# Residual rows and result kept with channels as rows, and parameter rows packed into two loads, in a two-layer diffusion backbone

## Chip, cores and metric

The kernel runs on one core of one Trainium2 chip. The metric is the device time of the core in microseconds (us) for one execution. The kernel before was timed in three runs: their median is 1773.47 us, the lowest 1773.41 and the highest 1774.19. One more execution was recorded by the hardware profiler: it took 1773.3 us.

## What is computed

The reference is a diffusion backbone of two layers over 512 latent tokens `x` (1, 512, 1024) with 256 context tokens `ctx` (1, 256, 1024). Cut to what matters:

```
for layer in 0, 1:
    mod, mod_c = silu(c) @ ada_w + ada_b, silu(c_ctx) @ ada_w + ada_b   # shift, scale, gate: twice 3 x 1024
    hx = rms_norm(x, norm1_g) * (1 + sc1) + sh1                          # hc alike, from ctx and mod_c
    yx, yc = windowed_gqa(hx, hc) if layer == 0 else hgrn2_bidir(hx, hc)
    x  = x + g1 * yx                                                     # the residual
    hx2 = rms_norm(x, norm2_g) * (1 + sc2) + sh2
    x  = x + g2 * conv_glu(hx2)                                          # 1024 -> 2 x 2816 -> 1024
    ctx = the same two steps, in layer 0 only
return x                                                                 # (1, 512, 1024)
```

Layer 0 mixes by attention: 16 heads in 4 groups, a window of 128 tokens on each side and all context keys in one softmax with a sink. Layer 1 mixes by a gated linear recurrence in both directions. All data is float32.

## The kernel before

**Layout.** TensorE contracts over the 128 partitions, so activations are kept with channels as partitions: the residual is `xl`, 8 channel tiles of 128 x 512 latent tokens, and `xc`, 8 tiles of 128 x 256 context tokens. `x` and `ctx` come, and the result goes, with tokens as rows, so three places of the program turn 128 x 128 blocks: PE multiplies the block with an identity (`ident`, the first half of the constant tile `cst`; the second half, `ones`, is a matrix of ones), and ACT or DVE copies the turned block from PSUM.

**Products.** For precision each float32 weight tile is split into a high and a low part: ACT writes the high part `wh` (L118, L142), DVE the rest, `wl` (L119, L143). Each product is then three matmuls (high by high, high by low, low by high), issued by `mm_steps` (L177), by `product` (L195) and, for the projections of attention, at L634.

**Start (`setup` from L199, `load_params`, `first_norm`).** ACT's queue loads `cst`. SP's queue loads six token tiles of 128 tokens x 1024 channels (L483: four of `x`, two of `ctx`). After the first of them `load_params` is called: it loads the rows of the small parameters (`c`, `c_ctx`, two norm gains, biases, convolution weights) into a tile `rows` by eleven DMAs, three on SP (L221 to L223) and eight on ACT (L224 to L230). Then SP loads 32 tiles `ar` of the modulation weights, 256 KB each (L303), and among these the weights `wr` of the key and value projection. The parameter rows are turned into columns (`par`), the conditioning `cs` is made of `c`, and PE works out the first modulation products (`ada`, L282). The token tiles are normalized in place. Then `flip` (L515) turns them, 6 blocks for each of the 8 channel tiles, 48 blocks in all (products named `n`), a modulation makes `hn` of them (L355 is one of its steps), and the first product that uses `hn` is `kv`.

**Attention.** For each of 4 groups and 6 query tiles: scores `S` on PE (L814), row maximum on DVE, exponential on ACT (L820), row scale `P` on POOL (L822), transposes `pt` on PE (L872), the products `pv` with the values (L882), and a copy to `o` on ACT (L884). Other projections are laid between these steps.

**Attention output (`attn_out` from L928).** For each pair of channel tiles d and d + 4 the two weight tiles are loaded and split. For each d, the 128 channels d of `x` and `ctx` are loaded a second time, with tokens as rows, into a tile `xs` (L937 and L938, on ACT's queue, in rows of 512 bytes), PE turns 6 blocks (L941, `xT`), ACT copies them to `xl` and `xc` (L943), and then come the 48 pairs of matmuls of the output projection `ao` (each pair 512 and 256 tokens wide). DVE adds the result, times the gate, onto `xl` and `xc` (L955). The attention output `oh` is itself split before (ACT L893, DVE L894). PSUM holds two tiles for `xT` and two for `ao`, each of two banks.

**Middle.** The convolutional GLU of layer 0, the recurrence of layer 1 and the second GLU follow, untouched by the change. The last products of the second GLU are `dn` (L177), which DVE adds onto `xl` (L1116; the last channel tile is added in two halves, L1111).

**Result (`done1`).** As each channel tile of `xl` is final, PE turns its four blocks (L1551; for the last channel tile two blocks for each half, L1543), ACT copies them from PSUM (L1552, L1544), and SP stores them with tokens as rows: three stores of two channel tiles each, one of one tile, and two halves of the last (L1556, L1554, L1545).

**What sets the order.** The program is written in the order above, but a list scheduler lays the instructions out anew for each engine, by a simulated timeline and by priorities; the order of rows below is its outcome. Each engine then executes its instructions in that order, and an instruction that waits holds all behind it. The DMAs of SP and ACT are instructions in their streams. Each DMA takes one of eight completion semaphores (DMAHW0 to DMAHW7 in the rows) in turn, and a DMA whose semaphore is still owed by an earlier DMA waits until that one has landed.

Of the kernel before, what the change touches and what calls it, by code (L numbers as in the profile page):

```python
# [8 lines left out]
F32 = mybir.dt.float32  # L9
# [64 lines left out]
class Kernel:  # L74
# [135 lines left out]
    def load_params(self, es):  # L210
# [5 lines left out]
        q = nc.scalar  # L216

        def rowsrc(x):
            return x.rearrange("l (r p) -> (l r) p", p=P)
# [5 lines left out]
        q.dma_start(out=rows[48:64, 0, :], in_=rowsrc(a["hgrn_lb_logits"]))  # L225
        q.dma_start(out=rows[64:65, 0, :], in_=rowsrc(a["hgrn_o_gain"]))
        q.dma_start(out=rows[0:96, 1, :], in_=rowsrc(a["ada_b"]))
        for l in range(2):
            q.dma_start(out=rows[0:66, 2 + l, :], in_=a["ffn_conv_w"][l].rearrange("w (r p) -> (w r) p", p=P))
            q.dma_start(out=rows[66:88, 2 + l, :], in_=a["ffn_conv_b"][l:l + 1].rearrange("w (r p) -> (w r) p", p=P))  # L230
# [239 lines left out]
    def first_norm(self, es, hn, psR, tables, after):  # L470
# [9 lines left out]
        for i in range(6):  # L480
            x = xp.tile([P, D], F32, tag="x", name=f"x{i}")
            src = a["x"][0, i * P:(i + 1) * P, :] if i < 4 else a["ctx"][0, (i - 4) * P:(i - 3) * P, :]
            nc.sync.dma_start(out=x, in_=src)  # L483
            xs.append(x)
            if i == 0:
                self.load_params(es)
# [441 lines left out]
    def attn_out(self, oh, hs, acc, tmp, pj, pp):  # L928
        nc, a = self.nc, self.a
        wout = a["attn_w_out"][0]  # L930
        for dp in range(KT // 2):
            w = self.load_w([self.wcols(wout, d * P, P) for d in (dp, dp + 4)])
            for j in range(2):
                d = dp + 4 * j
                xs = tmp.tile([P, 6, P], F32, tag="xs", name="xs")
                cs = slice(d * P, (d + 1) * P)
                nc.scalar.dma_start(out=xs[:, 0:4], in_=a["x"][0, :, cs].rearrange("(t p) c -> p t c", p=P))  # L937
                nc.scalar.dma_start(out=xs[:, 4:6], in_=a["ctx"][0, :, cs].rearrange("(t p) c -> p t c", p=P))  # L938
                pt = pp.tile([P, 1024], F32, tag="p2", name="xT")
                for i in range(6):  # L940
                    nc.tensor.transpose(pt[:, i * P:(i + 1) * P], xs[:, i], self.ident)  # L941
                for lo, hi, x in self.segs(False):
                    nc.scalar.activation(x[:, d], pt[:, lo:hi], AF.Copy)  # L943
# [485 lines left out]
    def run(self, stop=99):  # L1429
# [33 lines left out]
        with ExitStack() as e2:  # L1463
            pp, pj = (_Turn([self.pool(e2, f"{n}{i}", 1, PSUM) for i in range(2)]) for n in ("ppA", "pjA"))
            xsp = self.pool(e2, "xsp", 2)
            self.attn_out(oh, hs, acc, _Multi(tmp, xsp, ("xs",)), pj, pp)
# [67 lines left out]
        ost = {}  # L1534

        def done1(d, bank, part=None):

            if d == KT - 1:
                n = LAT // 2
                pt = bank("xo")  # L1540
                o = gp.tile([P, 2, P], F32, tag="g", name="osl")
                for i in range(2):
                    nc.tensor.transpose(pt[:, i * P:(i + 1) * P], self.xl[:, d, part * n + i * P:part * n + (i + 1) * P], self.ident)  # L1543
                nc.scalar.activation(o, pt[:, :n].rearrange("p (i c) -> p i c", c=P), AF.Copy)  # L1544
# [78 lines left out]
```

## Time and profile before

| | |
|---|---|
| median of three runs | 1773.47 us |
| profiled execution | 1773.3 us |
| span of its instructions | 1771.5 us |
| PE busy | 1742.6 us (98%), 13033 matmuls |
| DVE busy | 1308.5 us (74%) |
| ACT busy | 833.6 us (47%) |
| POOL busy | 247.3 us (14%) |
| DMA | 166.44 MB, 94 GB/s on average |

All times in the rows of the profile are microseconds from the first instruction; the span ends with the last one, and the execution's own time is 1.8 us longer. PE is the matrix engine, DVE the vector engine, ACT the scalar engine, POOL the GpSimd engine and SP an engine that only issues DMAs. `L515` is line 515 of the kernel before. Four kinds of rows are shown further on:

- A row of the chain or of the timeline: start, duration, engine, what was made, line, number of instructions in the row. The chain is followed back from the last instruction, at each step to what released it, or to the instruction before it on its engine. In a timeline the brackets at the end hold the idle time before the row and what ended it.
- A row of the windows: a stretch, its length, then for PE, PE's weight loads, DVE, ACT and POOL the busy time (and how many instructions), then the granted clock of PE (1.00 is full speed), the sum of the DMA engines' busy shares, and GB/s.
- A row of the groups: line, engine, operation, tile, count, then the mean, median and longest duration in ns, and when.
- A row of the waits: who waits for what, the time in sum, how often, the longest.

### The profile page before, as it was taken

What the parts mean: (1) busy time and instruction counts of PE and PEld (TensorE: products, weight loads), DVE (VectorE), ACT (ScalarE), POOL (GpSimd) and SP (SyncE); (2) the same over time, 40 slices, a digit from 0 to 9 for tenths busy, and PEclk for the clock granted to TensorE, in tenths of its full rate; (3) what the DMA queues carried; (4) which work ended last, traced back from release to release, by engine and by line L of the source; (5) the groups of instructions that cost most, each with busy time, mean ns of one, the idle gap of its engine ahead of it and who ended that gap; (6) DMA issues with size and microseconds to landing.
All of it is one profiled execution on the core that took longest, in us unless ns stands there. A gap on an engine that the chain in (4) does not pass through costs nothing.

```text
span 1771.5 us, 32299 instructions
## 1 busy us (share of the span) xinstructions
PE 1742.6 (98%) x13033; PEld 1528.3 (86%) x13033; DVE 1308.5 (74%) x2394; ACT 833.6 (47%) x1740; POOL 247.3 (14%) x232
## 2 busy tenths in 40 slices
PE   5999999999999999999999999999999999999998
PEld 4967775789889888999999889999897899999997
DVE  6576677477777776867867767777776699999984
ACT  4355556565534443534455333333333465565553
POOL 1133333200100110100100101111110001111110
PEclk9999999999999999999999999999999999999999
DMA  9351005133333343213114212121225423333311
GB/s 309 110 198 42 24 2 191 52 92 113 122 120 99 123 139 96 87 42 99 54 52 117 62 45 61 53 57 40 58 73 190 123 72 105 110 105 108 91 59 66
DMA packets 205188, 166.44 MB, mean 94 GB/s; under 512 B 5406, under 2 KB 199023, under 8 KB 199919
## 3 DMA queue, kind: packets, MB, share of 16 engines
q1 hardware_dynamic: 197376, 160.47, 29.5%
q10 hardware_dynamic: 7662, 3.92, 0.8%
q8 instruction: 102, 1.67, 0.4%
q14 instruction: 48, 0.39, 0.1%
HBM read 162.27 MB, written 2.10 MB: 93 GB/s over the span
## 4 chain that ended last, share of the span: by engine, by line
PE 96%; DMA 2%; DVE 1%; ACT 0%; issue 0%; POOL 0%; SPq 0%; ACTq 0%; DVEq 0%
PE dn L177 17%; PE pZ L195 17%; PE pV L195 8%; PE pf L177 8%; PE pY L195 4%; PE pjq L634 4%; PE pv L177 4%; PE ao L177 4%; PE pv L882 3%; PE pgate L177 3%; PE pq L177 3%; PE pt L872 3%; PE ada L316 2%; PE kv L634 2%; PE pd L969 2%; PE S L814 2%
## 5 line engine op out<-in xcount | busy, mean ns | idle before, releaser
L195 PE MATMUL pZ<-hs,wh 128*128 128x386 f32 (+1 forms) x1312 | 296.7, 314 | 0.0
L177 PE MATMUL dn<-g,wh 128*128 128x512 f32 (+1 forms) x1062 | 268.0, 356 | 0.0
L142 ACT ACTIVATE wh<-wr 128x512 fp32r<-128x512 f32 x246 | 153.7, 629 | 242.7 <-PE pZ L195 89.2
L118 ACT ACTIVATE wh<-wr 128x512 fp32r<-128x512 f32 (+2 forms) x204 | 120.2, 603 | 271.5 <-PE pf L177 82.1
L195 PEld LDWEIGHTS pZ<-hs,wh 128*128 128x128 f32 x1312 | 224.1, 189 | 14.8 <-ACT wh L142 5.9
L143 DVE TENSOR_TENSOR wl<-wr,wh 128x512 fp32r<-128x512 f32 x246 | 182.5, 746 | 35.8 <-ACT wh L142 31.6
L195 PE MATMUL pZ<-hs,wl 128*128 128x386 f32 (+1 forms) x656 | 204.7, 313 | 0.0
L177 PEld LDWEIGHTS dn<-g,wh 128*128 128x128 f32 x1062 | 174.7, 189 | 25.7 <-ACT g L1062 0.3
L119 DVE TENSOR_TENSOR wl<-wr,wh 128x512 fp32r<-128x512 f32 (+2 forms) x204 | 140.4, 695 | 74.3 <-ACT wh L118 65.1
L992 POOL TENSOR_TENSOR gg<-gg,R 128x772 f32<-128x772 f32 (+1 forms) x41 | 85.3, 2079 | 715.2 <-DVE gg L991 626.0
L177 PE MATMUL dn<-g,wl 128*128 128x512 f32 (+1 forms) x531 | 162.1, 355 | 0.0
L195 PE MATMUL pV<-hs,wh 128*128 128x386 f32 (+1 forms) x656 | 148.6, 313 | 0.0
L195 PEld LDWEIGHTS pZ<-hs,wl 128*128 128x128 f32 x656 | 123.4, 188 | 0.1
L177 PE MATMUL pf<-hn,wh 128*128 128x512 f32 (+1 forms) x512 | 117.7, 344 | 0.6 <-DVE gate L1160 0.6
L195 PEld LDWEIGHTS pV<-hs,wh 128*128 128x128 f32 x656 | 111.9, 189 | 1.3 <-issue 0.8
L195 PE MATMUL pV<-hs,wl 128*128 128x386 f32 (+1 forms) x328 | 102.2, 313 | 0.0
L177 PEld LDWEIGHTS dn<-g,wl 128*128 128x128 f32 x531 | 89.4, 188 | 14.2
L1116 DVE SCALAR_TENSOR_TENSOR xl<-dn,mod,xl 128x512 f32<-128x512 f32 x95 | 70.5, 745 | 29.6 <-PE dn L177 29.5
L177 PEld LDWEIGHTS pf<-hn,wh 128*128 128x128 f32 x512 | 79.4, 189 | 12.1 <-DVE gate L1160 0.8
L634 PE MATMUL pjq<-wh,hn 128*128 128x256 f32 x384 | 76.8, 289 | 0.0
L195 PE MATMUL pY<-hs,wh 128*128 128x386 f32 (+1 forms) x328 | 76.7, 314 | 0.0
L822 POOL TENSOR_SCALAR P<-P,r 128x512 f32<-128x512 f32 (+1 forms) x64 | 53.0, 832 | 95.8 <-DVE r L821 73.8
(321 smaller groups left out, 3895.9 us busy)
## 6 DMA issues: line engine op xcount, KB each, us to landing
wr<-in_ffn_w_up SPq DMA_DIRECT2D x88, 512.0 KB, 5.2
wada<-in_ada_w SPq DMA_DIRECT2D x40, 1024.0 KB, 5.0
wr<-in_hgrn_w_in SPq DMA_DIRECT2D x40, 512.0 KB, 5.1
ar<-in_ada_w SPq DMA_DIRECT2D x32, 256.0 KB, 7.0
wd<-in_ffn_w_down SPq DMA_DIRECT2D x16, 512.0 KB, 3.4
wr<-in_attn_w_in SPq DMA_DIRECT2D x6, 1024.0 KB, 8.5
wr<-in_ffn_w_down SPq DMA_DIRECT2D x12, 384.0 KB, 3.0
wr<-in_attn_w_out SPq DMA_DIRECT2D x8, 512.0 KB, 4.3
```

The lines of the kernel that those rows point to most:

```text
L118: nc.scalar.activation(wh, src, AF.Copy)
L119: nc.vector.tensor_tensor(wl, src, f(wh), op=ALU.subtract)
L142: nc.scalar.activation(ops[i][0], src, AF.Copy)
L143: nc.vector.tensor_tensor(ops[i][1], src, f(ops[i][0]), op=ALU.subtract)
L177: nc.tensor.matmul(o, lhsT=wt, rhs=at[:, t0:t0 + o.shape[1]], start=(first and n == 0 and i == 0), stop=(last and n == len(ks) - 1 and i = ...
L195: self.nc.tensor.matmul(ps, lhsT=wt, rhs=at, start=(first and k == 0 and i == 0), stop=(k == nk - 1 and i == 2), skip_group_check=not first)
L634: nc.tensor.matmul(out, lhsT=x, rhs=y[:, wk], start=(start and k == 0 and j == 0), stop=(stop and k == KT - 1 and j == 2))
L822: nc.gpsimd.tensor_scalar(p[:, :n], p[:, :n], r[:, j:j + 1], 1.0, op0=ALU.mult, op1=ALU.mult)
L872: nc.tensor.transpose(pt[:, j * P:(j + 1) * P], pr[j][:, b * P:(b + 1) * P], self.ident)
L882: nc.tensor.matmul(pv[a * HD:(a + 1) * HD, 0:256], lhsT=V[:, tiles[b], g, :], rhs=pT[:, a * 256:(a + 1) * 256], start=(b == 0), stop=(b == ...
L992: times = lambda eng, o, x, y: eng.tensor_tensor(o, x, y, op=ALU.mult)
L1116: nc.vector.scalar_tensor_tensor(x[:, d], o, self.modc(l, v, 5, d), x[:, d], op0=ALU.mult, op1=ALU.add)
```

## The change

Nothing of the arithmetic between the token tiles and the last addition is changed. Four things are:

1. The program's caller hands in two more inputs, `xT` (1024 x 512) and `ctxT` (1024 x 256), which are `x` and `ctx` with channels as rows. `attn_out` loads these straight into `xl` and `xc`: for each pair of channel tiles one DMA of 512 KB in rows of 2 KB and one of 256 KB in rows of 1 KB, eight DMAs on ACT's queue. The second loads `xs`, the 48 transposes and the sixteen copies go. The PSUM that the transposes had goes to `ao`: four tiles of two banks, taken in the order 0, 1, 2, 3, 2, 3, 0, 1.
2. The result leaves the kernel with channels as rows (1024 x 512), and the caller turns it. `done1` stores each channel tile of `xl` directly, the last in two halves: nine stores. Its 32 transposes, its copies and its staging tiles go.
3. The caller packs the parameter rows into one input `rows`. `load_params` loads it with two DMAs on ACT's queue, of 65 rows and of 3 x 96 rows. It is called after the third token tile is issued, not after the first.
4. Only the identity half of `cst` is loaded; the ones are written by a memset on DVE.

The core of the diff:

```diff
     def setup(self):
-        nc.scalar.dma_start(out=cst, in_=a["cst"][:, C_ID:C_ID + 2 * P])
+        nc.scalar.dma_start(out=cst[:, 0:P], in_=a["cst"][:, C_ID:C_ID + P])
+        nc.vector.memset(cst[:, P:2 * P], 1.0)
...
     def load_params(self, es):
-        nc.sync.dma_start(out=rows[0:8, 0, :], in_=rowsrc(a["c"]))
-        nc.sync.dma_start(out=rows[8:16, 0, :], in_=a["c_ctx"].rearrange("(r p) -> r p", p=P))
-        nc.sync.dma_start(out=rows[16:32, 0, :], in_=rowsrc(a["norm1_g"]))
-        q.dma_start(out=rows[32:48, 0, :], in_=rowsrc(a["norm2_g"]))
...
+        nc.scalar.dma_start(out=rows[0:65, 0, :], in_=a["rows"][0, 0:65])
+        nc.scalar.dma_start(out=rows[0:96, 1:4, :], in_=a["rows"][1:4, 0:96].rearrange("b r c -> r b c"))
...
     def first_norm(self, es, hn, psR, tables, after):
             nc.sync.dma_start(out=x, in_=src)
-            if i == 0:
+            if i == 2:
                 self.load_params(es)
...
     def attn_out(self, oh, hs, acc, tmp, pj):
             w = self.load_w([self.wcols(wout, d * P, P) for d in (dp, dp + 4)])
+            for x, src in ((self.xl, a["xT"]), (self.xc, a["ctxT"])):
+                nc.scalar.dma_start(out=x.rearrange("p (j d) t -> p j d t", j=2)[:, :, dp],
+                                    in_=src.rearrange("(j d p) t -> p j d t", j=2, p=P)[:, :, dp])
             for j in range(2):
                 d = dp + 4 * j
-                xs = tmp.tile([P, 6, P], F32, tag="xs", name="xs")
-                cs = slice(d * P, (d + 1) * P)
-                nc.scalar.dma_start(out=xs[:, 0:4], in_=a["x"][0, :, cs].rearrange("(t p) c -> p t c", p=P))
-                nc.scalar.dma_start(out=xs[:, 4:6], in_=a["ctx"][0, :, cs].rearrange("(t p) c -> p t c", p=P))
-                pt = pp.tile([P, 1024], F32, tag="p2", name="xT")
-                for i in range(6):
-                    nc.tensor.transpose(pt[:, i * P:(i + 1) * P], xs[:, i], self.ident)
-                for lo, hi, x in self.segs(False):
-                    nc.scalar.activation(x[:, d], pt[:, lo:hi], AF.Copy)
                 ps = pj.tile([P, 1024], F32, tag="pj", name="ao")
...
-            pp, pj = (_Turn([self.pool(e2, f"{n}{i}", 1, PSUM) for i in range(2)]) for n in ("ppA", "pjA"))
+            pj = [self.pool(e2, f"pjA{i}", 1, PSUM) for i in range(4)]
+            self.attn_out(oh, hs, acc, tmp, _Turn(pj + 2 * pj[2:]))
...
         def done1(d, bank, part=None):
-            pt = bank("xo")
-            for i in range(NQ):
-                nc.tensor.transpose(pt[:, i * P:(i + 1) * P], self.xl[:, d, i * P:(i + 1) * P], self.ident)
-            nc.scalar.activation(ost[0][:, :, (d % 2) * P:(d % 2) * P + P], pt[:, :LAT].rearrange("p (i c) -> p i c", c=P), AF.Copy)
...
+            c = slice(0, LAT) if part is None else slice(part * LAT // 2, (part + 1) * LAT // 2)
+            nc.sync.dma_start(out=a["out"][d * P:(d + 1) * P, c], in_=self.xl[:, d, c])
```

The scheduler lays the whole program out anew. In the rows below `x_131<-in_x 128x1024` is a token tile (the numbers are the compiler's), brackets name the semaphores that an instruction waits for, and `x3` means three alike. The lines are those of each kernel's own file; the changed one is up to 37 lines shorter.

SP at the very start of the program, before:

```order
L483 DMA x_108<-in_x 128x1024
L221 DMA rows<-in_c 8x128
L222 DMA rows<-in_c_ctx 8x128
L223 DMA rows<-in_norm_g 16x128
L483 DMA x_127<-in_x 128x1024 [waits DMAHW0_49]
L483 DMA x_129<-in_x 128x1024 [waits DMAHW2_49]
L483 DMA x_131<-in_x 128x1024 [waits DMAHW4_49]
L483 DMA x_133<-in_ctx 128x1024 [waits DMAHW6_49]
```

and SP at the same place, changed:

```order
L471 DMA x_109<-in_x 128x1024
L471 DMA x_111<-in_x 128x1024
L471 DMA x_113<-in_x 128x1024
L471 DMA x_123<-in_x 128x1024
L471 DMA x_125<-in_ctx 128x1024 [waits DMAHW0_49]
L471 DMA x_127<-in_ctx 128x1024 [waits DMAHW2_49]
L291 DMA ar<-in_ada_w 128x2x256 [waits DMAHW4_49]
```

DMAHW0 belongs to `cst`, the first DMA of the program, in both. Before, the second token tile waits for it; now the fifth one does.

PE, before, in the rows that lead to its first `kv` product; 28 of the 48 token transposes (`n`) stand ahead of it, the last four of which are here:

```order
L515 MATMUL n_407<-cst,x_108 128x128 [waits DVE_49]
L515 MATMUL n_407<-cst,x_127 128x128
L515 MATMUL n_407<-cst,x_129 128x128
L515 MATMUL n_407<-cst,x_131 128x128
L634 MATMUL kv<-wh,hn_73 128x256 [waits Activation_49]
```

and PE changed, where 46 of them stand ahead of the first `kv`:

```order
L503 MATMUL n_429<-cst,x_109 128x128 [waits DVE_49]
L503 MATMUL n_429<-cst,x_111 128x128
L503 MATMUL n_429<-cst,x_113 128x128
L503 MATMUL n_429<-cst,x_123 128x128
L270 MATMUL ada_476<-ar,cs 32x128 [waits DMAHW4_49]
L270 MATMUL ada_476<-ar,cs 32x128 x3
L270 MATMUL ada_476<-ar,cs 32x128 [waits DMAHW5_49]
L270 MATMUL ada_476<-ar,cs 32x128 x3
L622 MATMUL kv<-wh,hn_74 128x256 [waits Activation_49]
```

Some modulation products (`ada`) now also stand between the last of these transposes and `kv`.

ACT at the end of attention, before; `o` is the last copy of attention, `y<-mod` a small step of the modulation:

```order
L884 ACTIVATE o<-pv 128x2x128 [waits PE_49]
L383 ACTIVATE y<-mod_123 128x2 [waits DVE_49,Activation_49,Pool_49]
L383 ACTIVATE y<-mod_123 128x2
L937 DMA xs<-in_x 128x4x128 [waits DMAHW4_49,DMAHW5_49,DMAHW0_49,PE_49]
L893 ACTIVATE oh<-o 128x768 [waits Activation_49]
L893 ACTIVATE oh<-o 128x768
L938 DMA xs<-in_ctx 128x2x128 [waits DMAHW1_49]
L118 ACTIVATE wh<-wr 128x512 [waits DVE_49]
L118 ACTIVATE wh<-wr 128x512
L943 ACTIVATE xl<-xT 128x512
L943 ACTIVATE xc<-xT 128x256
```

and ACT there, changed:

```order
L872 ACTIVATE o<-pv 128x2x128 [waits PE_49]
L922 DMA xc<-in_ctxT 128x2x256 [waits DVE_49,DMAHW1_49,Activation_49,Pool_49]
L118 ACTIVATE wh<-wr 128x512 [waits PE_49]
L881 ACTIVATE oh<-o 128x768 [waits Activation_49]
L881 ACTIVATE oh<-o 128x768
L371 ACTIVATE y<-mod_119 128x2 [waits DMAHW5_49]
L371 ACTIVATE y<-mod_119 128x2
L922 DMA xc<-in_ctxT 128x2x256 [waits DMAHW2_49]
L922 DMA xc<-in_ctxT 128x2x256 x2
L118 ACTIVATE wh<-wr 128x512 [waits DMAHW5_49,DVE_49]
L118 ACTIVATE wh<-wr 128x512
L922 DMA xl<-in_xT 128x2x512 x2
```

The loads of `xs` stood before and between these rows; now the first load of `xc` stands behind the last `o` copy and waits for DVE, ACT and POOL, the other context loads come behind the split of `oh`, and the latent loads behind a pair of `wh`.

PE at the very end of the program, before; `xo` are the transposes of the result:

```order
L177 MATMUL dn<-g,wl 128x256
L1551 MATMUL xo<-cst,xl 128x128 [waits DVE_49]
L1551 MATMUL xo<-cst,xl 128x128 x3
L1543 MATMUL xo<-cst,xl 128x128 [waits DVE_49]
L1543 MATMUL xo<-cst,xl 128x128
L1543 MATMUL xo<-cst,xl 128x128 [waits DVE_49]
L1543 MATMUL xo<-cst,xl 128x128
```

The rows of the changed kernel end with `dn` products; on SP the stores of `xl` follow, each behind an addition on DVE.

More of the change, by code (lines that the diff above doesn't have):

```diff
@@ L926, in attention, with attn_out @@
         return ohs[0]
-    def attn_out(self, oh, hs, acc, tmp, pj, pp):
+    def attn_out(self, oh, hs, acc, tmp, pj):
         nc, a = self.nc, self.a
@@ L1533, in run @@
         rows = self.row_factor(acc, True, tmp, bk, "ps", 512, R, -1.0)
-        ost = {}
         def done1(d, bank, part=None):
-            if d == KT - 1:
-                n = LAT // 2
-                pt = bank("xo")
[L1541 to L1544, printed above, removed]
-                nc.sync.dma_start(out=a["out"][0, part * n:part * n + n, d * P:(d + 1) * P].rearrange("(t p) c -> p t c", p=P), in_=o)
-                return
-            if d % 2 == 0:
-                ost[0] = gp.tile([P, NQ, 256], F32, tag="g", name="ost")
-            pt = bank("xo")
-            for i in range(NQ):
-                nc.tensor.transpose(pt[:, i * P:(i + 1) * P], self.xl[:, d, i * P:(i + 1) * P], self.ident)
-            nc.scalar.activation(ost[0][:, :, (d % 2) * P:(d % 2) * P + P], pt[:, :LAT].rearrange("p (i c) -> p i c", c=P), AF.Copy)
-            if d == KT - 2:
-                nc.sync.dma_start(out=a["out"][0, :, d * P:(d + 1) * P].rearrange("(t p) c -> p t c", p=P), in_=ost[0][:, :, 0:P])
-            elif d % 2:
-                nc.sync.dma_start(out=a["out"][0, :, (d - 1) * P:(d + 1) * P].rearrange("(t p) c -> p t c", p=P), in_=ost[0])
+            c = slice(0, LAT) if part is None else slice(part * LAT // 2, (part + 1) * LAT // 2)
+            nc.sync.dma_start(out=a["out"][d * P:(d + 1) * P, c], in_=self.xl[:, d, c])
         self.ffn(1, hs, R, rows, True, tmp, acp, bk, gp, done1)
@@ L1614 @@
     data["cst"] = shape_constants()
+    rows = [[data[n] for n in ("c", "c_ctx", "norm1_g", "norm2_g", "hgrn_lb_logits", "hgrn_o_gain")], [data["ada_b"]]]
+    rows += [[data["ffn_conv_w"][l], data["ffn_conv_b"][l]] for l in range(2)]
+    data["rows"] = np.zeros((4, P, P), np.float32)
+    for b, parts in enumerate(rows):
+        v = np.concatenate([x.reshape(-1) for x in parts])
+        data["rows"][b].reshape(-1)[:v.size] = v
+    for n in ("c", "c_ctx", "norm1_g", "norm2_g", "hgrn_lb_logits", "hgrn_o_gain", "ada_b", "ffn_conv_w", "ffn_conv_b"):
+        del data[n]
+    data["xT"] = np.ascontiguousarray(data["x"][0].T)
+    data["ctxT"] = np.ascontiguousarray(data["ctx"][0].T)
     for n, x in data.items():
@@ L1617 @@
         args[n] = nc.dram_tensor(f"in_{n}", x.shape, mybir.dt.from_np(x.dtype), kind="ExternalInput").ap()
-    args["out"] = nc.dram_tensor("out_0", (1, LAT, D), F32, kind="ExternalOutput").ap()
+    args["out"] = nc.dram_tensor("out_0", (D, LAT), F32, kind="ExternalOutput").ap()
     with tile.TileContext(nc, schedule_with_timeline_sim=True) as tc:
@@ L1621 @@
     r = run_bass_kernel_spmd(nc, [arrays], core_ids=[0])
-    return r.results[0]["out_0"]
+    return np.ascontiguousarray(r.results[0]["out_0"].T)[None]
```

16 lines of the change are left out of this document (removed).

## The prediction

> **What bounds the kernel now.** I read the page first: busy shares, then shares of the chain that ended last.
>
> ```profile
> PE 1742.6 (98%) x13033; PEld 1528.3 (86%) x13033; DVE 1308.5 (74%) x2394; ACT 833.6 (47%) x1740; POOL 247.3 (14%) x232
> PE 96%; DMA 2%; DVE 1%; ACT 0%; issue 0%; POOL 0%; SPq 0%; ACTq 0%; DVEq 0%
> ```
>
> PE is the bound nearly everywhere, so an instruction taken out of its stream shortens the run, and work taken from ACT does not. The 2% of DMA in the chain sits mostly at the start. So I read the chain there, the windows, the waits of PE and of the load queue SP, and the timeline of ACT.
>
> ```profile
> 0.73 4.01 DMA cst<-in_cst
> 6.12 6.91 DMA x<-in_ctx
> 13.05 5.28 DMA ar<-in_ada_w
> 18.34 8.46 DMA wr<-in_attn_w_in
> ```
> ```profile
> 3.00:4.00 1.00, 0.00 (x0) 0.00 (x0) 0.00 (x0) 0.00 (x0) 0.00 (x0) 1.00 0.97 360
> 4.00:5.00 1.00, 0.00 (x0) 0.00 (x0) 0.23 (x1) 0.00 (x0) 0.00 (x0) 1.00 0.10 29
> 5.00:6.00 1.00, 0.05 (x1) 0.08 (x1) 0.00 (x0) 0.00 (x0) 0.00 (x0) 1.00 0.54 131
> 6.00:7.00 1.00, 0.68 (x2) 0.29 (x2) 0.60 (x4) 0.28 (x2) 0.00 (x0) 1.00 0.88 311
> 7.00:8.00 1.00, 0.04 (x1) 0.00 (x0) 0.45 (x4) 0.98 (x2) 0.00 (x0) 1.00 0.74 273
> ```
> ```profile
> 15.00:20.00 5.00, 3.36 (x35) 1.31 (x35) 4.35 (x19) 2.41 (x5) 0.75 (x1) 1.00 0.91 287
> 20.00:25.00 5.00, 3.95 (x39) 2.20 (x40) 4.40 (x19) 1.15 (x1) 1.65 (x1) 1.00 0.95 315
> 40.00:45.00 5.00, 5.00 (x72) 3.81 (x64) 3.31 (x9) 1.77 (x3) 1.68 (x2) 1.00 1.10 348
> ```
> ```profile
> SPq L483 <- DMA cst<-in_cst: 2.5, 1, 2.5
> PE ada L282 <- DMA ar<-in_ada_w: 11.2, 6, 9.3
> ```
> ```profile
> 26.83 2.19 ACT L118 ACTIVATE wh<-wr 128x512 fp32r<-128x512 f32 x4 [1.05 <-DMA wr<-in_attn_w_in]
> 29.19 0.83 ACT L355 ACTIVATE hn<-ny 128x768 fp32r<-128x768 f32 x1
> ```
>
> The last column of the windows is GB/s. Data flows at about 350, but there is a hole from 4 to 8 us: SP had issued one token tile and three 4 to 8 KB rows, and its next token tile waited 2.5 us for cst. The chain then runs through loads to 26.8 us, where ACT splits the first weights and after them the first normalized tile (29.19). From there PE does not stop: 5.00 of 5 us.
>
> **The change part by part.** One profiled execution of 1773.3 us (span 1771.5, 1.8 around it) carries the sum; the median of the runs, 1773.47, is 0.17 above it.
>
> *Start.* Eleven small loads become two, and all four latent tiles are issued before SP has to wait. Filling the hole: (350-29)+(350-131)+(350-311)+(350-273) GB/s over 1 us each is 656 KB, at 350 GB/s 1.9 us. From 15 to 25 us the loads run at 287 and 315, which misses 63*5+35*5 = 490 KB or 1.4 us, while SP's turns come behind small loads of ACT that are issued late. Those now go early; I take half, 0.7. So the first weights land 1.9 to 3.3 us earlier. Moreover the order puts 46 of the 48 token transposes ahead of PE's first kv product, where 28 stood: 18 at 0.11 us (priced below) are 2.0 us of PE work moved into time in which PE waits anyway. Against it, ACT now has two channel groups of copies between the weight split and hn, one more than before. All gains would give 5.3; with some new stalls I take **-3.5**, from -5.5 to 0. The ones half of cst, now a DVE memset, is nothing: DVE is idle for most of the first 4 us. The packed rows hold back the conditioning only if they land after the first ada weights, 13 us away.
>
> [...] cst now shares the DMA engines with 2 MB of tokens instead of 0.5 MB, and the fifth token tile waits for cst. If cst came behind all of it (2.1 MB at 350 GB/s after 2.2 us: 8.2 us) the hole would move, not close, and the 1.9 be lost. [...] No row here has such a load beside 2 MB.
>
> *Attention output.*
>
> ```profile
> 354.43 0.87 PE xT L941 x8
> 399.79 0.66 PE xT L941 x6
> 400.44 8.44 PE ao L177 x48
> 409.31 5.39 DMA wr<-in_ffn_w_up
> ```
> ```profile
> L941 PE MATMUL xT<-cst,xs x48: 270/272/328, 332.3 to 400.2; 128*128 128x128 f32 x48
> ```
>
> Six transposes stand in the chain for 0.66 us, 0.11 each (272 ns is the latency of one). All 48, in eight groups, are 8*0.66 = **-5.3**. 40 of them stand in the chain (-4.4, the low end); -6.0 if each also cost a little of its neighbour. The sixteen ACT copies that go were not on the path and are worth nothing. Behind this stage the chain goes on with a load that starts when the last ao product frees its space; that moves with PE.
>
> The transposed rows come in eight loads on ACT's queue: a new wait. The first needs the last attention results; behind it ACT holds a weight split and the split of oh, for which PE waits.
>
> ```profile
> 332.30 1.85 POOL L822 TENSOR_SCALAR Pc<-Pc,r 128x256 f32<-128x256 f32 x4 [4.41 <-DVE r L821]
> 346.75 1.15 ACT L118 ACTIVATE wh<-wr 128x512 fp32r<-128x512 f32 x2 [1.16 <-DVE oh L894]
> 351.17 0.75 DVE L955 SCALAR_TENSOR_TENSOR xl<-ao,mod,xl 128x512 f32<-128x512 f32 x1 [0.51 <-PE ao L177]
> ```
>
> POOL's last result is there at 334, long before ACT's turn (the last o copy, some 343), so that wait costs 0. The latent loads stand behind the wh pair, 347.9. With 1 MB of context rows ahead (2.9 us at 350 GB/s) and about 3 us of their own, the first lands near 351 to 354, for an addition that now starts at 351.17: up to 3 us late. PE does not feel it: four product tiles in PSUM instead of two let it run through two further groups of 8.4 us. Without that cover it would cost the 3 us.
>
> *Result.*
>
> ```profile
> 1752.12 0.57 PE xo L1551 x4
> 1762.81 0.44 PE xo L1551 x4
> 1763.25 2.12 PE dn L177 x18
> 1765.37 0.45 PE xo L1551 x4
> 1765.85 0.60 ACT ost L1552
> ```
> ```profile
> 1765.41 0.48 DVE L1111 SCALAR_TENSOR_TENSOR xl<-dn,mod,xl 128x256 f32<-128x256 f32 x1 [0.58 <-PE dn L177]
> 1767.19 0.92 SPq L1545 DMA_DIRECT2D out<-osl  x2
> ```
>
> Six groups of four transposes stand before the last dn products: 0.57+5*0.44 = 2.8 us. After them the last half tile is added by 1765.89 and its store is the second of the pair at 1767.19 to 1768.11, so at about 1767.6. Now the store follows the addition directly, at about 1766.0: 1.6 us. Together **-4.4**; -3.6 if the final wait does not shrink with the store, -5.0 if 2 KB rows also land sooner than 512 byte ones.
>
> *Attention between.* The scheduler has laid out PE, DVE and ACT anew from the start to 330 us, though no instruction there changes. PE changes from one kind of product to another 401 times before ao, where it was 392.
>
> ```profile
> 318.24 0.65 PE L882 MATMUL pv<-pT,V 128*64 128x256 f32 x4
> 318.82 0.66 PE L872 MATMUL pt<-cst,P 128*128 128x128 f32 x4
> 80.00:120.00 40.00, 39.05 (x321) 29.97 (x319) 31.42 (x82) 20.80 (x44) 14.03 (x13) 1.00 0.44 169
> 280.00:328.50 48.50, 47.51 (x346) 29.05 (x345) 34.02 (x79) 31.23 (x79) 18.59 (x26) 1.00 0.29 85
> 317.36 0.69 ACT L820 ACTIVATE P<-S,nm 128x513 f32<-128x513 f32 x1 [0.82 <-DVE nm L845]
> ```
>
> Four pv take 0.58 from start to start where 4*0.117 (half of the 0.231 that a product of 512 columns takes in 18 halves of 2.12) make 0.47: some 0.11 per change of kind, nine more are **+1.0**. PE's idle time here is 0.95+0.99, so a better order gains at most 1.9. How much a worse one costs no row bounds; I take +3 as the end of the ordinary.
>
> Sum: -3.5-5.3-4.4+1.0 = -12.2. 1773.3 becomes 1761.1; on the median 1773.47 it is 1761.3.
>
> **Rivals.** (a) *The start gives nothing*, cst's lateness moving the hole: 1761.3+3.5 = 1764.8. For it: SP's wait on cst stays. [...] 0.12.
>
> (b) *The new order in attention costs* more, 5 to 8 us: 1767 to 1769. For it: hundreds of moved rows; against it, the same scheduler left PE 1.9 us idle there. 0.09.
>
> (c) *PE starts cold.*
>
> ```profile
> 16.37 0.66 PE L282 MATMUL ada<-ar,cs 128*32 128x128 f32 x8 [9.34 <-DMA ar<-in_ada_w]
> 27.60 0.43 PE L282 MATMUL ada<-ar,cs 128*32 128x128 f32 x8 [0.22 <-DMA ar<-in_ada_w]
> ```
>
> The same eight products took 0.66 us early and 0.43 later, though the clock column reads 1.00 in both windows. If the pause before kv now leaves PE in the early state, the first 36 products (4.2 us) take 0.66/0.43 as long: 2.3 us more, 1763.6. [...] 0.06.
>
> (d) *Slower.* The place is the 24 attention blocks (4 groups, 6 query tiles). If the new order lost the work that covers the exponentials, PE would wait one of them (0.69) in each block: 24*0.69 = 16.6, 1777.9. It decides from 15.7/24 = 0.65 us a block. Against it: PE waits there less than 2 us in all. 0.03.
>
> (e) *The output stage is not PE's*: the weight splits set its pace and the 5.3 comes back as waits, with the other terms small: 1768 to 1772. For it: ACT and DVE feed each product. Against it: the ao groups run 8.44 us for 48 pairs of products without a gap. 0.04.
>
> **How the numbers follow.** My forecast has 0.66: **1761.3 us**. Its low end takes the three gains at their better ends (-5.5-6.0-5.0) and half of PE's idle time in attention (-0.95): 1756.0. Its high end takes the worse ends (0-4.4-3.6) with the +1.0: 1766.5. With (a), (c) and half of (b) 1756 to 1768 holds the time 8 times in 10. About 0.2%, 3.5 us, is what a measurement here can tell from no change. Faster: 0.66+0.12+0.08+0.06 = 0.92. Same, from (b) and (e): 0.04. Slower, (d) and what I overlook: 0.04.
>
> **What the changed profile would show.** Right: no window between 4 and 8 us under 250 GB/s, and the first weight split (26.83 now) 2 to 3 us earlier; ao groups following each other within 0.1 us; the last store within 0.3 us of the last addition; PE's idle time from 80 to 328 us under 4 us. Wrong: SP waiting for cst with the windows empty, PE waiting on xl or wh in ao, or attention longer by over 3 us. A time above 1768 would mean that a whole term is missing.

## The result, and the profile after

The changed kernel takes 1760.52 us (median of four runs, 1760.47 to 1760.90) where the kernel before takes 1773.66 (four runs, 1773.41 to 1774.19): the ratio is 0.9926, with an interval from 0.9913 to 0.9938. That is 13.1 us less; the forecast was 1761.3, 12.2 less than 1773.47. The profiled execution took 1760.5 us, of which its span is 1758.7.

The page of the changed kernel, its busy shares and the shares of the chain:

```profile
PE 1732.2 (98%) x12953; PEld 1519.5 (86%) x12953; DVE 1308.4 (74%) x2395; ACT 824.7 (47%) x1715; POOL 247.2 (14%) x232
PE 94%; DVE 2%; DMA 2%; POOL 1%; ACT 0%; issue 0%; ACTq 0%; SPq 0%; DVEq 0%; POOLq 0%
```

PE has 10.4 us less to do and is still the bound. DVE and POOL have gained a per cent each of the chain. About half of what DVE gained lies at the start, as is seen below; the rest of it, and most of POOL's, comes behind the start, in attention.

**Where the time went.** A tile's view gives the first and last start of its instructions, so the last product of each kind marks the end of a stage. For the kernel before, the last product of attention's scores (`Sc`), of the attention output (`ao`), the last `pZ` and the last `dn`:

```profile
L814 PE MATMUL Sc<-KB,qT x32: 276/280/363, 144.5 to 328.1; 128*128 128x256 f32 x32
L177 PE MATMUL ao<-oh,wl x128: 279/337/400, 333.7 to 408.6; 128*128 128x512 f32 x64, 128*128 128x256 f32 x64
L195 PE MATMUL pZ<-hs,wl x656: 276/333/346, 411.9 to 1743.4; 128*128 128x386 f32 x88, 128*128 128x258 f32 x76
L177 PE MATMUL dn<-g,wl x531: 277/392/483, 473.0 to 1765.1; 128*128 128x512 f32 x114, 128*128 128x256 f32 x63
```

and for the changed kernel:

```profile
L802 PE MATMUL Sc<-KB,qT x32: 274/281/387, 144.8 to 326.5; 128*128 128x256 f32 x32
L177 PE MATMUL ao<-oh,wl x128: 274/336/400, 330.2 to 401.6; 128*128 128x512 f32 x64, 128*128 128x256 f32 x64
L195 PE MATMUL pZ<-hs,wl x656: 276/333/346, 404.9 to 1736.3; 128*128 128x386 f32 x88, 128*128 128x258 f32 x76
L177 PE MATMUL dn<-g,wl x531: 276/392/404, 465.9 to 1755.0; 128*128 128x512 f32 x114, 128*128 128x256 f32 x63
```

The same rows of the profiles of four experiments give the other columns of this table. Each line is a stage in us, from the mark above it; in brackets is the difference to before.

| stage ends with | before | changed | start alone | attention output alone | result alone | two `ao` tiles |
|---|---|---|---|---|---|---|
| last `Sc` | 328.1 | 326.5 (-1.6) | 325.9 (-2.2) | 330.9 (+2.8) | 328.1 (0) | 327.3 (-0.8) |
| last `ao` | 80.5 | 75.1 (-5.4) | 80.5 (0) | 75.1 (-5.4) | 80.6 (+0.1) | 81.4 (+0.9) |
| last `pZ` | 1334.8 | 1334.7 (-0.1) | 1335.9 (+1.1) | 1334.9 (+0.1) | 1335.5 (+0.7) | 1333.9 (-0.9) |
| last `dn` | 21.7 | 18.7 (-3.0) | 21.7 (0) | 21.7 (0) | 18.7 (-3.0) | 18.7 (-3.0) |
| end of the span | 6.4 | 3.7 (-2.7) | 6.5 (+0.1) | 5.8 (-0.6) | 3.7 (-2.7) | 3.4 (-3.0) |

The span is 12.8 us shorter: 1.6 from the start and attention, 5.4 in the attention output, 5.7 at the end, and 0.1 in 1335 us of middle, which no edit touches. That middle also tells how far one execution can be from another there: up to 1.1 us.

**The start.** The windows of the changed kernel over the hole that the loads had, GB/s in the last column:

```profile
4.00:5.00 1.00, 0.00 (x0) 0.00 (x0) 0.00 (x0) 0.02 (x1) 0.00 (x0) 1.00 1.06 420
5.00:6.00 1.00, 0.34 (x1) 0.18 (x1) 0.23 (x1) 1.00 (x2) 0.00 (x0) 1.00 0.97 377
6.00:7.00 1.00, 0.00 (x0) 0.00 (x0) 0.52 (x1) 0.13 (x2) 0.00 (x0) 1.00 1.07 404
7.00:8.00 1.00, 0.00 (x0) 0.00 (x0) 0.97 (x4) 0.00 (x0) 0.00 (x0) 1.00 1.03 376
```

The hole is gone. Yet the first `kv` product comes at 32.24 us, and it was 31.24 before. Three rows of the timeline of ACT, and the row of PE with that product:

```profile
9.88 0.33 ACTq L599 DMA_DIRECT2D sink<-in_attn_sink  x1
10.26 0.22 ACT L241 ACTIVATE sg<-par 128x16 f32<-128x16 f32 x1 [4.13 <-DMA rows<-in_rows]
...
24.32 2.18 ACT L118 ACTIVATE wh<-wr 128x512 fp32r<-128x512 f32 x4
```
```profile
32.24 0.39 PE L622 MATMUL kv<-wh,hn 128*128 128x256 f32 x1
```

The weights are there sooner: ACT splits the first of them at 24.32, where it was 26.83. But ACT stands still from 6.13 to 10.26 us. The first row says why. The load of `sink`, 8 KB that nobody needs before attention, is an instruction in ACT's stream, and its semaphore is the one of the second packed parameter load. ACT waits until that has landed, and the square sums of the token tiles wait behind it. Three rows of the chain that leads there:

```profile
1.86 8.00 DMA rows<-in_rows
9.88 0.33 ACTq L599
...
11.80 1.77 POOL rs L456
```

The packed load is on its way for 8.0 us, beside 2 MB of token tiles. The first row factor `rs` comes only then, and the normalization, the transposes and `hn` come after it. Such a hold is not new. In the kernel before, three loads of ACT (the table `tb` and two gains) waited in the same way for parameter rows, and ACT stood from 7.98 to 12.55 us:

```profile
12.55 1.06 ACT L499 ACTIVATE sq<-x 128x1024 f32<-128x1024 f32 x1 [4.58 <-DMA rows<-in_ffn_conv_w]
13.98 1.76 POOL L468 TENSOR_TENSOR rs<-rv,mh 128x3 f32<-128x3 f32 x1 [12.94 <-DVE rv L467]
```

So the change did not make the row factor late: it begins at 11.80 where it began at 13.98. But before, the chain went through the loads of weights, which landed later still; now it goes through this hold. And from 20.27 us, when the second set of token tiles begins to be ready, PE works without a pause until the first `kv` product, with 46 transposes and more modulation products to do first. The busy time of PE alone in the first 35 us, before and changed:

```profile
0.00:35.00 35.00, 17.14 (x172) 1.00 0.90 298
0.00:35.00 35.00, 18.63 (x197) 1.00 0.98 325
```

PE stands idle 16.4 us there where it was 17.9. That is 1.5 us less, about what the start gave.

**The attention output and the end.** From the chain of the changed kernel:

```profile
344.10 57.77 PE ao L177 x328
...
402.30 5.29 DMA wr<-in_ffn_w_up
...
1736.61 18.67 PE dn L177 x90
...
1755.30 0.48 DVE xl L1093
```

328 of the 384 `ao` products stand in one row of the chain, without a gap, and the load behind them moves with PE, 402.30 for 409.31. At the end nothing stands between the `dn` products, and behind them is only the addition. What DVE had to wait for at its first addition, and the issues of the nine stores on SP (timeline):

```profile
354.30 0.75 DVE L937 SCALAR_TENSOR_TENSOR xl<-ao,mod,xl 128x512 f32<-128x512 f32 x1 [4.36 <-DMA xl<-in_xT]
1749.63 6.51 SPq L1519 DMA_DIRECT2D out<-xl  x9
```

### The profile page after: what moved, and what is told of

Read it like the earlier page. It is cut to its first block, busy times and chain, and to the rows that moved or that the text cites. A ratio compares the mean times of both kernels' runs of the same rounds, so it can differ in the third digit from the quotient of the medians.

```text
span 1758.7 us, 32100 instructions
## 1 busy us (share of the span) xinstructions
PE 1732.2 (98%) x12953; PEld 1519.5 (86%) x12953; DVE 1308.4 (74%) x2395; ACT 824.7 (47%) x1715; POOL 247.2 (14%) x232
## 4 chain that ended last, share of the span: by engine, by line
PE 94%; DVE 2%; DMA 2%; POOL 1%; ACT 0%; issue 0%; ACTq 0%; SPq 0%; DVEq 0%; POOLq 0%
PE dn L177 18%; PE pZ L195 17%; PE pV L195 8%; PE pf L177 8%; PE pY L195 4%; PE pv L177 4%; PE ao L177 4%; PE pjq L622 3%; PE pgate L177 3%; PE pv L870 3%; PE pq L177 3%; PE pt L860 2%; PE kv L622 2%; PE ada L304 2%; PE ho L177 2%; PE pd L951 2%
## 5 line engine op out<-in xcount | busy, mean ns | idle before, releaser
L177 PE MATMUL pf<-hn,wl 128*128 128x512 f32 (+1 forms) x256 | 66.0, 339 | 0.0
```

What stands on the lines that cost most here:

```text
L177: nc.tensor.matmul(o, lhsT=wt, rhs=at[:, t0:t0 + o.shape[1]], start=(first and n == 0 and i == 0), stop=(last and n == len(ks) - 1 and i = ...
```

## The experiments

The first three kernels have one part of the change each, the fourth undoes one; the others test what their profiles left open.

**The start alone**, on the kernel before: half of `cst`, the two packed loads, `load_params` behind the third token tile.

```diff
-        nc.sync.dma_start(out=rows[0:8, 0, :], in_=rowsrc(a["c"]))
...
+        nc.scalar.dma_start(out=rows[0:65, 0, :], in_=a["rows"][0, 0:65])
+        nc.scalar.dma_start(out=rows[0:96, 1:4, :], in_=a["rows"][1:4, 0:96].rearrange("b r c -> r b c"))
```

> The kernel before with the start alone changed: half of cst, packed parameter rows, token tiles ahead of them. The changed kernel's trace is 1.6 us ahead of the one before when the last scores of attention are done (326.7 against 328.3 us). Theory: that is what the start gives, so 1773.5 - 1.6 = 1771.9 us, with the first kv product near 32.2 us though the first weight split comes near 24.3, because ACT stands still from 6.1 to 10.3 us behind its load of sink. Rival: the start gives the 3.5 us of the forecast and the other edits' new order in attention took part of it back: 1770.0 us.

Measured: 1773.07 us (1772.21 to 1774.57, ten runs) against 1774.25 for the kernel before beside it, ratio 0.9991 (0.9981 to 1.0000). At the last `Sc` its trace is 2.2 us ahead, of which it loses 1.1 in the untouched middle. Its first `kv` product comes at 31.64, 0.6 earlier than expected, but the wait is the same as in the changed kernel:

```profile
10.17 0.22 ACT L241 ACTIVATE sg<-par 128x16 f32<-128x16 f32 x1 [4.14 <-DMA rows<-in_rows]
```

So without the other edits, too, the start does not give 3.5 us: it gives some 2 by the trace and 1.2 by the medians, whose interval reaches 1.0000. The rival, that the other edits took a part back, could claim the 0.6 us between 2.2 and 1.6, less than two executions differ by elsewhere.

**The attention output alone**, on the kernel before.

```diff
+            for x, src in ((self.xl, a["xT"]), (self.xc, a["ctxT"])):
+                nc.scalar.dma_start(out=x.rearrange("p (j d) t -> p j d t", j=2)[:, :, dp], ...)
...
-                    nc.tensor.transpose(pt[:, i * P:(i + 1) * P], xs[:, i], self.ident)
```

> The kernel before with the attention output alone changed: residual loaded with channels as rows, no transposes, four product tiles in PSUM. Theory: 48 transposes in eight groups of 0.66 us, 5.3 us, so 1768.2 us, and PE runs the ao groups without a gap. Rival: as soon as the order is laid out anew, attention moves too, by about 1 us either way: 1767.2 or 1769.2 us.

Measured: 1768.51 us (1768.02 to 1770.20, five runs), ratio 0.9966 (0.9953 to 0.9980), 5.7 us less. The stage itself shows 5.4 less. But this trace, the longest of the five runs, is 2.8 us late at the last `Sc`, although PE's instructions are in the same order as before up to the last of attention. The windows of its start (PE's busy time first, the granted clock third from the end), and two rows of PE:

```profile
26.00:28.00 2.00, 0.93 (x14) 0.54 (x12) 1.02 (x4) 1.07 (x3) 1.64 (x2) 1.00 1.10 365
28.00:30.00 2.00, 1.48 (x18) 0.87 (x12) 2.00 (x5) 2.00 (x5) 0.00 (x0) 0.73 1.10 348
30.00:32.00 2.00, 2.00 (x20) 0.80 (x20) 2.00 (x4) 1.29 (x4) 0.00 (x0) 0.50 1.13 355
...
34.00:36.00 2.00, 2.00 (x16) 1.28 (x15) 0.46 (x2) 0.00 (x0) 0.00 (x0) 0.56 1.10 347
```
```profile
27.69 0.42 PE L282 MATMUL ada<-ar,cs 128*32 128x128 f32 x8 [1.07 <-DMA ar<-in_ada_w]
30.11 0.66 PE L282 MATMUL ada<-ar,cs 128*32 128x128 f32 x8
```

PE waited 1.07 us for a modulation weight, and for some more pieces after it. From 28.9 us its granted clock is 0.50 until about 35.8, and the same eight products take 0.66 in place of 0.42. The last `kv` product comes at 79.5 us where it came at 76.7. This is the forecast's rival (c), in another kernel: the profile of the kernel before, with the same order of PE, kept its clock here, and this one lost it. The kernel before, too, had runs of up to 1778.7 us beside these experiments, where its lowest was 1772.5; whether the clock is the cause there is not shown. The changed kernel had none above 1761.82 in nine.

**The result alone**, on the kernel before.

```diff
+            c = slice(0, LAT) if part is None else slice(part * LAT // 2, (part + 1) * LAT // 2)
+            nc.sync.dma_start(out=a["out"][d * P:(d + 1) * P, c], in_=self.xl[:, d, c])
```

> The kernel before with the result alone changed: channels as rows stored from the residual. The two traces differ by 5.7 us behind the last pZ product (3.0 to the last dn product, 2.7 behind it). Theory: all of that belongs to this edit: 1767.8 us. Rival: the forecast's 4.4 us is right and the other 1.3 come from a different order of dn and pZ that the other edits bring: 1769.1 us.

Measured: 1768.39 us (1767.54 to 1770.31, five runs), ratio 0.9966 (0.9952 to 0.9980), 5.9 less than the 1774.25 beside it. Its trace is 3.0 us shorter up to the last `dn` and 2.7 behind it, just as the changed kernel's, and the other stages agree within the 1.1 us of before. The 5.7 belong to this edit.

**Two `ao` tiles in PSUM**, in the changed kernel, in place of four.

```diff
-            self.attn_out(oh, hs, acc, tmp, _Turn(pj + 2 * pj[2:]))
+            self.attn_out(oh, hs, acc, tmp, _Turn(pj[:2]))
```

> The changed kernel with two product tiles in PSUM for ao in place of four. In the changed kernel the first addition onto xl waits 4.4 us for its load and starts at 354.3 us, where the one before started at 351.2. Theory: four tiles hide this, and with two PE must wait at the third group for about the 3 us by which the addition is late: 1763.5 us. Rival: PE has enough other work there or the addition is early enough, no change: 1760.5 us.

Measured: 1765.00 us (1761.70 to 1766.56, four runs), ratio 0.9942 (0.9927 to 0.9957). The profiled execution is the longest of them, and its `ao` stage takes 81.4 us where four tiles take 75.1: 6.3 more, twice the expected price. By the medians the price is 4.5 us, and the shortest run is only 1.2 above the changed kernel, so the 6.3 hold for this execution alone. The one wait of PE in that stage, and the windows around it:

```profile
PE ao L177 <- DVE xc L937: 3.7, 1, 3.7
```
```profile
352.00:354.00 2.00, 0.07 (x1) 0.00 (x0) 0.41 (x1) 0.39 (x1) 0.00 (x0) 1.00 0.93 323
354.00:356.00 2.00, 0.27 (x1) 0.30 (x2) 1.56 (x3) 0.77 (x2) 0.00 (x0) 0.57 0.99 324
356.00:358.00 2.00, 2.00 (x7) 1.72 (x7) 2.00 (x6) 2.00 (x6) 0.00 (x0) 0.50 1.09 340
...
360.00:362.00 2.00, 2.00 (x10) 1.69 (x10) 1.85 (x3) 0.95 (x3) 0.00 (x0) 0.73 0.12 36
```

PE waits for the late addition 3.7 us, and then works at a granted clock of 0.50 until 361: seven products from 356 to 358 us, where it does thirteen from 362 to 364 at 1.00. To tell the wait from the clock, the next kernel fills the wait.

**Two tiles, with the wait filled**: sixteen products added ahead of the third group, into a PSUM tile that nobody reads.

```diff
+            if dp == 1:
+                ps = fill.tile([P, 1024], F32, tag="pj", name="fill")
+                for i in range(16):
+                    nc.tensor.matmul(ps[:, 0:512], lhsT=w[0][0][0][:, 0:P], rhs=oh[:, 0, 0, 0:512], start=True, stop=True)
```

> The kernel with two product tiles for ao, with 16 matmuls of 512 columns added ahead of the third group of products, whose result nobody reads (3.7 us of work, as long as the wait there). With two tiles PE waited 3.7 us and then ran at a granted clock of 0.50 for 6.6 us; together some 6.3 us. Theory: the second part is the clock alone, which falls because PE pauses; with the pause filled the clock stays at 1.00 and the time is 2.5 us below the two-tile kernel with its pause, so the changed kernel's 1760.5 + 3.7 = 1764.2 us, where the two-tile kernel's profiled execution took 1766.5. Rival: the clock is lowered for another reason (the loads, or the pause being too long already) or the filling only adds: 1766.5 us or more.

Measured: 1764.00 us (1763.69 to 1764.54, five runs), ratio 0.9941 (0.9927 to 0.9954). The same windows:

```profile
352.00:354.00 2.00, 2.00 (x11) 1.65 (x10) 0.51 (x1) 0.48 (x1) 0.00 (x0) 1.00 0.96 329
354.00:356.00 2.00, 1.88 (x9) 1.18 (x7) 1.12 (x3) 0.34 (x1) 0.00 (x0) 1.00 0.94 346
```

The clock stays at 1.00 with the same late load, and work that is of no use takes 2.0 us off the longest run (1764.54 for 1766.56), although the load came 0.4 us later here. That agrees with the windows: of the 6.3 us, 3.7 were the wait, and from 355.7 to 361 PE worked 5.3 us at a clock of 0.50, which by estimate (half of 5.3) loses 2.6. The two-tile runs without the filling spread over 4.9 us, those with it over 0.9. What the filling gains in time is less clear: 1.0 us by the medians, whose ranges overlap, and the shortest run without it, 1761.70, beats all runs with it. So the two traces show what this pause did to the clock, 0.50 with it and 1.00 with it filled, and not that the filling pays.

**The changed kernel again**, for comparison:

> The changed kernel once more, to have it on the chip of the runs beside it: 1760.5 us by the runs so far, or up to 3 us more in runs in which PE loses its clock near the start, as the start in the run with the attention output alone showed.

Measured: 1760.98 us (1760.64 to 1761.82, five runs), ratio 0.9925 (0.9912 to 0.9937). The mean granted clock is 1.000 in all five.

**The load of `sink` on SP**, in the changed kernel.

```diff
-        nc.scalar.dma_start(out=s0, in_=a["attn_sink"][0:1, :].broadcast_to([P, NH]))
+        nc.sync.dma_start(out=s0, in_=a["attn_sink"][0:1, :].broadcast_to([P, NH]))
```

> The changed kernel with the load of sink (8 KB) issued by SP in place of ACT. Theory: ACT stood from 6.1 to 10.3 us only because this load, in its stream, waited for the semaphore of the second packed rows load (landed at 9.9); without it the first normalization is up to 4 us earlier, the first kv product comes near 29.5 us in place of 32.2, and the time falls by 2 to 3 us, to 1758 us. Rival: the first modulation weights, which land until 24 us, set hn and so kv anyway: 1760.5 us, no change. Second rival: PE does its transposes earlier and then waits for the modulation in pieces, the granted clock falls before kv, and it is slower, 1761 to 1763 us.

Measured: 1759.68 us (1759.03 to 1759.85, four runs), ratio 0.9916 (0.9902 to 0.9929): 1.3 less than the changed kernel beside it, with no overlap of the runs, about half of what was expected. The chain shows what took over:

```profile
1.88 8.36 DMA rows<-in_rows
...
10.37 0.41 PE pr L232
10.80 0.26 DVE par L233
11.06 0.07 DVE rv L455
```

ACT no longer waits for the packed load, but DVE does: the copy of the turned bias rows stands in its stream ahead of `rv`, the first step of the row factor. The wait has gone from one engine to the next, and the row factor begins 0.5 us earlier than with ACT held (11.55).

**The packed load split as well**: the 96 bias rows first, the convolution rows by themselves.

```diff
-        nc.scalar.dma_start(out=rows[0:96, 1:4, :], in_=a["rows"][1:4, 0:96].rearrange("b r c -> r b c"))
+        nc.scalar.dma_start(out=rows[0:96, 1, :], in_=a["rows"][1, 0:96])
+        nc.scalar.dma_start(out=rows[0:88, 2:4, :], in_=a["rows"][2:4, 0:88].rearrange("b r c -> r b c"))
```

> The changed kernel with sink loaded by SP and the second packed load split in two, first the 96 rows of the modulation bias, then the convolution rows. With sink alone moved, DVE's copy of the turned bias rows waited for the packed load until 10.2 us and the first row factor behind it began at 11.1. Theory: the bias rows now land near 6 us, the normalizations come 1.3 us or more earlier again, PE, which worked without a pause from 19.0 us to kv, starts earlier by as much, and the time falls from 1759.7 to 1758.4 us. Rival: the modulation weights, which land until 24 us, or the token tiles set the pace, no change against 1759.7 us.

Measured: 1759.12 us (1757.81 to 1759.39, four runs), ratio 0.9913 (0.9898 to 0.9928). The bias rows land later than expected, at 8.0 us, and ACT is held again until then, by the load of a gain whose semaphore is theirs; but the chain moves:

```profile
1.86 6.11 DMA rows<-in_rows
...
9.66 0.18 DVE rv L456
```

The row factor begins 1.4 us earlier than with `sink` moved alone, and the first `kv` product comes at 28.1 us in place of 31.9. What is left of that at the last `Sc` is 1.2 us (323.6 against 324.8), and in the medians 0.6. The two medians are from different sets of runs, so the split alone is not clear of noise; both edits together are: all four runs are below all nine of the changed kernel, and the last `Sc` comes 2.9 us earlier than there (323.6 for 326.5).

**PE kept busy ahead of the transposes**, in the changed kernel: 30 transposes that nobody reads.

```diff
+            fill(14, self.par[:, P:P + 96])
+            fill(16, xs[2][:, 0:P])
```

> The changed kernel with 30 transposes added on PE between 10.8 and some 16 us, whose result nobody reads, so that PE is busy ahead of the token transposes. In the changed kernel PE worked without a pause from 20.3 us to the first kv product at 32.2, and until about 25 us the eight modulation products took 0.66 us, afterwards 0.43. Theory: PE is cold until 25 us and that sets the start; with PE warm the stretch from 20.3 to 25 takes half as long, kv comes near 30 us, and the time falls by 2 to 2.5 us to 1758.3 us. Rival: the modulation weights, which land until 24 us, and the copies of the transposes set hn anyway: within 0.5 us of 1760.7 us. Second rival: the added work delays the real transposes: up to 1763 us.

Measured: 1763.65 us (1760.45 to 1764.45, five runs), ratio 0.9933 (0.9921 to 0.9946), slower than the changed kernel. The profiled execution is the longest. Its windows:

```profile
18.00:20.00 2.00, 0.40 (x16) 0.13 (x7) 1.72 (x8) 0.51 (x1) 1.46 (x1) 1.00 1.05 354
20.00:22.00 2.00, 1.70 (x15) 1.25 (x15) 1.91 (x5) 0.64 (x1) 0.00 (x0) 0.79 1.10 363
22.00:24.00 2.00, 2.00 (x21) 0.70 (x19) 0.61 (x3) 0.98 (x2) 0.00 (x0) 0.50 1.09 351
```

The filling did make PE quick: at 20.56 us eight modulation products took 0.42 where the changed kernel needs 0.65. But PE still waited 1.9 us for the second normalization, and the clock fell to 0.50 from 21.2 to 24.6. The expected gain was lost there, by the thing that it was to cure: the last `kv` product comes at 74.7 us, 0.2 before that of the changed kernel. The second rival's cause, delayed transposes, is not excluded as a part of it. What makes this execution longer comes later. At the last `Sc` it is 2.5 us behind the changed kernel (329.0 for 326.5), and between the two marks PE waits for a modulation weight, as the changed kernel does for 1.2 us, and loses the clock once more:

```profile
PE ada L304 <- DMA wada<-in_ada_w: 2.8, 1, 2.8
```
```profile
104.00:108.00 4.00, 2.41 (x15) 1.54 (x16) 1.94 (x5) 1.09 (x4) 1.11 (x1) 0.81 0.96 373
108.00:112.00 4.00, 4.00 (x23) 2.04 (x21) 2.89 (x7) 2.50 (x7) 0.69 (x1) 0.76 0.89 348
```

Why that load is later here (it takes 6.2 us on its way, where it takes 4.7 in the changed kernel) is not shown.

**Both together**, the split loads and the filling (16 and 16 transposes):

> Both edits of the two runs beside it: sink on SP, the packed load split, and 32 transposes added on PE ahead of the token transposes. If each is right by itself and the two add up: 1758.4 - 2.3 = 1756.1 us. If the loads set the pace: 1758 to 1760 us.

Measured: 1758.59 us (1756.40 to 1761.39, five runs), ratio 0.9909 (0.9897 to 0.9922). The profiled execution is the shortest. Eight modulation products take 0.43 us there already at 18.51 us. It keeps its clock, its first `kv` product comes at 27.8 us, and it takes 1756.4 us. The theory's sum, 1756.1, is met, but not by its terms: the split's own profiled execution took 1757.8 and not 1758.4, and the filling is worth 1.4 us against it, not 2.3. The two shortest runs, 1756.4 and 1756.7, have a mean granted clock of 1.000, the other three, 1758.6 to 1761.4, one of 0.999 or 0.998; so the median gains nothing that is clear over the split alone. The best version that holds its time is the changed kernel with `sink` on SP and the packed load split, 1759.1 us.

## Why the prediction was right, and where not

The time, 1760.5, lies 0.8 us from the forecast and within its range. The mechanisms were right for the attention output and the result. That the sum came so near is in part luck: the start gave less than forecast and the result more, by about as much.

- **Start, -3.5, with attention's +1.0: -2.5 together. Measured -1.6.** The loads did what was said: the hole closed, and the first weight split came 2.5 us earlier, within the 1.9 to 3.3 worked out. `cst`, 64 KB now, landed 4.4 us after its issue, at about 5.1 us, although four token tiles were issued beside it; before, with 128 KB and one token tile beside it, it took 4.01 us and landed at 4.74. Rival (a) did not happen. That it was unlikely was the author's estimate, which no run had shown beforehand.
- **The step that failed** is the sentence that "The packed rows hold back the conditioning only if they land after the first ada weights, 13 us away". They landed at 9.9, and that was enough, not by the conditioning but through the queue: the `sink` load, eight DMAs further on, shares their semaphore, and ACT stood behind it. The prediction followed the queue of SP at the start and not that of ACT, where the same hold stood before as well (4.58 us). The chain of before went through loads up to the split, so the work between the tokens and `hn` had slack that was not measured. With the loads 2.5 us earlier, and the hold over only 2.3 us earlier, that work became the chain. The runs with `sink` moved, and then the load split, show the two waits one behind the other; without them the last `Sc` comes 2.9 us earlier, which is more than the start fell short.
- **The 18 transposes moved ahead of `kv`, 2.0 us.** They were to go into time in which PE waits anyway. From 20.27 us to `kv` there is no such time, and over the first 35 us the start saves 1.5 us of waiting in all: `kv` begins 1.0 us later than before, and its last product is 1.8 us earlier (74.9 for 76.7 us).
- **Attention, +1.0.** In two of the windows PE's idle time was 0.95 + 0.99 before; in the changed kernel

```profile
80.00:120.00 40.00, 38.43 (x311) 28.11 (x312) 32.01 (x83) 20.14 (x42) 13.55 (x12) 1.00 0.46 171
120.00:160.00 40.00, 39.86 (x313) 31.15 (x311) 25.90 (x68) 20.98 (x55) 14.24 (x18) 1.00 0.20 67
280.00:326.90 46.90, 45.76 (x344) 28.55 (x344) 34.02 (x78) 30.66 (x77) 18.40 (x25) 1.00 0.33 102
```

  it is 1.57 + 0.14 + 1.14 = 2.85, so 0.9 more. That is the forecast's size, but not its mechanism: it was priced by changes of product kind, which are busy time, and this is waiting, most of it for a modulation weight (1.2 us, 1.0 before), for an exponential (1.1, before 0.9) and for normalized keys (0.3, before none). Nor does it stand in the time: from the last `kv` to the last `Sc` product it was 251.4 us and is 251.6. So the term of +1.0 was too high by 0.8, if that stretch is what it meant, and what made up for the waits is not shown.
- **Attention output, -5.3. Measured -5.4**, in both kernels that have the edit. (A group is 48 matmuls, so 24 pairs, and not 48 pairs as the text further up has it; the 8.44 us are right.) The addition was late by 3.1 us (354.30 for 351.17), as said, and PE did not feel it. That cover was priced at 3 us if it were gone; without it the profiled execution lost 6.3, because PE's clock was 0.50 behind its pause of 3.7 us, and the median 4.5.
- **Result, -4.4. Measured -5.7**, beyond the better end of -5.0. The transposes gave 3.0 for 2.8. Behind the last product it was 2.7 for 1.6. From the end of the last addition to the end of the last store's issue it was 2.22 us (1765.89 to 1768.11) and is 0.36 (1755.78 to 1756.14), 1.9 less; from there to the end of the span it was 3.4 and is 2.6, 0.8 less. The first half is the term as forecast, with the issue of the store counted in full. The second half was held to be possible, 2 KB rows landing sooner, and not taken; that the row length is its cause was not tried apart.
- **Rivals.** (c), the cold PE, was given 0.06 and a price of 2.3 us. It did not happen in the changed kernel, whose `kv` products take 0.28 us each from the second one on (0.41 at a clock of 0.50 with the attention output alone), but at the start of two others: the granted clock was 0.50 from 28.9 to 35.8 us with the attention output alone, and from 21.2 to 24.6 with PE kept busy. With the attention output alone the last `kv` product was 2.8 us late, the pauses included. (a), (b), (d) and (e) did not happen.
- **The signs.** All of those named came true: no window under 250 GB/s, the split 2 to 3 us earlier, groups without a gap, the store directly behind the addition, idle time under 4 us. The one for the start said nothing about `kv`, which is where the start failed.

## What to carry to other kernels

A load that shortens the way to the first weights only counts if the work between the first data and the first product is not next (here the weights were split 2.5 us earlier, and 1.6 us came of it): look at the order of the compute engines' queues for small loads that nobody needs yet, whose semaphore belongs to a big one, as that of `sink`, 8 KB, belonged to 144 KB here and held ACT for 4.13 us. A wait of PE can cost clock afterwards, here an estimated 2.6 us on top of 3.7 in the execution that was profiled, where the two further PSUM tiles of the changed kernel spare it both. Where an edit takes work out of the bound engine in the middle of its stream, counting instructions by the chain's own rows gave the time within 0.1 us in 5.4.

## What the runs showed of the hardware

- The granted clock fell to 0.50 behind these pauses of PE: some 2.2 us into one of 3.7 us (two `ao` tiles); after one of 1.9 us and after one of 2.8 (PE kept busy at the start); and after pieces of 1.07, 0.33 and 0.19 us within 2.5 (attention output alone). It came back 6.8, 3.4, 3.4 and 6.8 us later, with PE at work in most of that time (5.3 of the 6.8 us with two `ao` tiles). Not every pause did this: a single one of 1.2 us in the changed kernel, and of 1.5 us with `sink` on SP, both for a modulation weight between 80 and 120 us, left the clock at 1.00.
- In the kernel before and the changed one the clock column reads 1.00 in all windows of the start, also where eight modulation products take 0.66 us and not 0.43 (until about 25 us). With the attention output alone the same eight took 0.66 where the column read 0.50. With PE kept busy from 10.77 us they took 0.42 at 20.56 already, at 1.00. So at the start of these kernels a reading of 1.00 stood beside both durations; why is not shown.
- A load of 144 KB in rows of 512 bytes, issued at 1.86 us beside token tiles of 2 MB, took 8.0 us (changed kernel); its first third by itself, issued at 1.86 us as well, took 6.1 (packed load split).
